# GLA scores as packed 64x64 products with a state per chunk, and low parts and rotary sums on VectorE

## The chip, the cores and the metric

The kernel runs on one core of one Trainium2 chip. The metric is the device time of one execution in microseconds. Before the change three runs took 1275.5, 1276.38 and 1276.91 us (median 1276.38).

## The reference

One layer of a streaming encoder over 1024 frames of width 1024, batch 1. A conditioning vector gives shift, scale and gate for two sublayers. The first sublayer mixes tokens:

```
u    = LN0(x) * (1 + scale1) + shift1
proj = u @ w_in                                 # 3600 columns: rq rk rv rg gq gk gv gg glr
ro   = head_norm(retention(rope(rq), rope(rk), rv)) * silu(rg)   # 4 heads, dk = dv = 128
go   = head_norm(gla(gq, gk, gv, log_a)) * silu(gg)              # 4 heads, dk = 64, dv = 128
x    = LN1(alpha * x + gate1 * ([ro | go] @ w_out))
```

The second is a feed-forward layer with a squared relu. All mixing is causal by chunks of 64 frames. The part that the change rewrites most is gated linear attention (GLA). With b the cumulative log gate inside a chunk, for each chunk and head:

```
A[t, s] = sum_d q[t, d] k[s, d] exp(-|b[t, d] - b[s, d]|)        # inside a chunk, both ways
o       = A @ v + (q * exp(b)) @ state
state   = exp(b_last) * state + (k * exp(b_last - b)).T @ v
```

The decay differs for each channel d, so A is not one matrix product.

## The kernel before

All arithmetic is float32. Large matmuls are computed from a high part (float32r, written by a cast on ScalarE, L205) and a low part (the rest, a subtraction, L206), three matmuls for one product (L211 to L213). The helper `split` does both; its argument `lo_eng` names the engine of the low part, GpSimd where it is missing. Before the change the low parts of w_in (`wl`: 52 tiles of 128x512 and 8 of 128x272, L206 called from `load_w`), those of every second half of the input (`ul`, 8 tiles, from `modulate`) and of every first half of w_out (`ol`, 8 tiles, from `load_out`) are on GpSimd.

The sequence is cut into two halves of 512 frames (h), the four GLA heads into two blocks of two heads (blk), which lie on partitions 0 to 63 and 64 to 127. `gla` is thus called four times, each time for 512 frames and two heads, between the projections. It works with tiles of 128 frames, which hold two chunks each. To build A it splits the pairs (t, s) of a tile by levels: at the level of u frames (32, 16, 8, 4, 2, 1) the pairs that lie in the two halves of a block of 2u frames are one product of `qe` and `ke`, both scaled with the exponential of b's distance from the boundary between the halves (E: GpSimd L562 and L563, exponential on ScalarE L564, products on VectorE L566 and L567). `scores` then does 8 matmuls of 64 channels, 128 keys and 128 queries (L544), into one PSUM bank for each head, and VectorE copies what belongs to this level over `am` by a mask (L552, two copies of 128x512 for each level). Two more calls of `scores` come first: one, with `qB` and `kB`, for pairs in which the query's chunk follows the key's (mask C_M64, L554), and one, with q and k, for the diagonal.

The state is kept for each tile of 128 frames. So `qB` and `kB`, scaled towards their own chunk's bounds, are turned by GpSimd into `qI` and `kI`, scaled towards the tile's bounds (L576, L577), with the tile's decay `gdt` (L580). `kI` is transposed and copied out (L583, L585), its product with v gives the update of each tile (L593), VectorE chains the states (L600), and the output is the sum of the product of `qI` with the state (L611) and that of `am` with v (L617).

In retention each of four heads' q and k is rotated: ScalarE copies the projection (L646), VectorE does three products (L647 to L649), GpSimd adds (L650), 16 times in all, and scales q with the decay (L654).

Instructions stand in the program as the functions call each other, but a planner then orders every engine's queue by priority and modelled times before the kernel runs, and gives tags without a fixed number of buffers what room there is. On the chip each engine works through its queue in that order. Weight tiles of w_in share 16 buffers (tag W) for their high and low parts. All loads and stores go through SP's queue.

Of the kernel before, what the change touches and what calls it, by code (L numbers as in the profile page):

```python
# [16 lines left out]
P = 128  # L17
# [21 lines left out]
C_TRI = 128  # L39
C_DEC = 256  # L40
C_QD = C_DEC + 512
C_M64 = C_QD + 512
C_LV = C_M64 + 128
LEVELS = (32, 16, 8, 4, 2, 1)
C_KD = C_LV + 128 * len(LEVELS)
C_N = C_KD + 4


# [3 lines left out]
def shape_constants():  # L52

    half = 64
    inv = (1.0 / (np.float32(10000.0) ** np.linspace(0.0, 1.0, half, dtype=np.float32))).astype(np.float32)
    ang = np.arange(SEQ, dtype=np.float32)[None, :] * inv[:, None]
    cos = np.cos(ang.astype(np.float64)).astype(np.float32)
    sin = np.sin(ang.astype(np.float64)).astype(np.float32)
    cosT = np.concatenate([cos, cos], 0)
    sinT = np.concatenate([sin, -sin], 0)  # L60
    lg = np.log1p(-(2.0 ** (-5.0 - np.arange(4, dtype=np.float64))))
    i = np.arange(P)
    s, t = i[:, None], i[None, :]
# [8 lines left out]
    c[:, C_M64:C_M64 + P] = (s < 64) & (t >= 64)  # L72
    for n, h in enumerate(LEVELS):
        c[:, C_LV + P * n:C_LV + P * (n + 1)] = (s // (2 * h) == t // (2 * h)) & (s // h != t // h)
# [5 lines left out]
def layer_kernel(ctx: ExitStack, tc, x, c, w_ada, b_ada, w_in, ret_norm_w, gla_gate_w, gla_gate_b,  # L80
# [55 lines left out]
    def table(o, n=P):  # L136
        return keep[:, o:o + n] if o < C_DEC else cst1[:, o - C_DEC:o - C_DEC + n]
# [212 lines left out]
    def load_w(ranges, kk):  # L350

        n = sum(r[1] for r in ranges)
        hi, lo = [], []
        for k in range(0, NK, kk):
            w = stage((P, kk, n))
            o = 0
            for a, m in ranges:
                nc.sync.dma_start(out=w[:, :, o:o + m], in_=wi[:, k:k + kk, a:a + m])
                o += m
            th, tl = S((P, kk, n), F32R, "wh"), S((P, kk, n), F32R, "wl")  # L360
            split(w, th, tl)
# [170 lines left out]
        return q, k, b, eb, qB, kB  # L532

    def gla(blk, h, gv, q, k, b, eb, qB, kB):
        am = [S(n="am"), S(n="am")]

        def scores(ka, qa, put):

            heads = [slice(64 * hd, 64 * hd + 64) for hd in range(2)]
            tiles = [slice(j * P, (j + 1) * P) for j in range(4)]  # L540
            pss = [mxt(), mxt()]
            for o in tiles:
                for hd in range(2):
                    T.matmul(pss[hd][:, o], lhsT=ka[heads[hd], o], rhs=qa[heads[hd], o], start=True, stop=True)  # L544
            for hd in range(2):
                put(am[hd].rearrange("p (j t) -> p j t", t=P), pss[hd].rearrange("p (j t) -> p j t", t=P))

        def cmask(o):
            return table(o).unsqueeze(1).broadcast_to([P, 4, P])

        def overlay(o):
            return lambda a, ps: V.copy_predicated(out=a, mask=cmask(o).bitcast(U32), data=ps)  # L552

        scores(kB, qB, lambda a, ps: V.tensor_tensor(out=a, in0=ps, in1=cmask(C_M64), op=ALU.mult))  # L554
        scores(k, q, overlay(C_ID))
        for n, u in enumerate(LEVELS):
            e = S(n="E")
            bv = b.rearrange("p (n u) -> p n u", u=2 * u)
            ev = e.rearrange("p (n u) -> p n u", u=2 * u)
            nb = HALF // (2 * u)  # L560
            ref = bv[:, :, u - 1:u].broadcast_to([P, nb, u])
            G.tensor_tensor(out=ev[:, :, :u], in0=ref, in1=bv[:, :, :u], op=ALU.subtract)  # L562
            G.tensor_tensor(out=ev[:, :, u:], in0=bv[:, :, u:], in1=ref, op=ALU.subtract)  # L563
            A.activation(e, e, AF.Exp)  # L564
# [3 lines left out]
            scores(ke, qe, overlay(C_LV + P * n))  # L568


        eb4 = eb.rearrange("p (j c u) -> p j c u", c=2, u=CHUNK)
        qI, kI = S(n="qI"), S(n="kI")
        for src, dst, c0 in ((qB, qI, 0), (kB, kI, 1)):
            s4 = src.rearrange("p (j c u) -> p j c u", c=2, u=CHUNK)
            d4 = dst.rearrange("p (j c u) -> p j c u", c=2, u=CHUNK)
            G.tensor_copy(out=d4[:, :, c0, :], in_=s4[:, :, c0, :])  # L576
            G.tensor_tensor(out=d4[:, :, 1 - c0, :], in0=s4[:, :, 1 - c0, :],  # L577
                            in1=eb4[:, :, c0, CHUNK - 1:CHUNK].broadcast_to([P, 4, CHUNK]), op=ALU.mult)
        dt = small(4, "gdt", bufs=4)
        G.tensor_tensor(out=dt, in0=eb4[:, :, 0, CHUNK - 1], in1=eb4[:, :, 1, CHUNK - 1], op=ALU.mult)  # L580
        kp = mxt()
        for j in range(4):
            T.transpose(out=kp[:, j * P:(j + 1) * P], in_=kI[:, j * P:(j + 1) * P], identity=ident)  # L583
        kt = S(n="kt")
        A.copy(out=kt, in_=kp)  # L585

        steps = range(4 if h == 0 else 3)
        before = [gstate[blk]]
        up = mxt((P, 4, P))
        for j in steps:  # L590
            vt = gv[2 * h + j // 2][:, j % 2, :]
            for hd in range(2):
                T.matmul(up[64 * hd:64 * hd + 64, j, :], lhsT=kt[:, j * P + 64 * hd:j * P + 64 * hd + 64],  # L593
                         rhs=vt[:, hd * P:(hd + 1) * P], start=True, stop=True)
        states = S((P, 4, P), n="states")
        for j in steps:
            if before[j] is None:
                V.tensor_copy(out=states[:, j, :], in_=up[:, j, :])
            else:
                V.scalar_tensor_tensor(out=states[:, j, :], in0=before[j], scalar=dt[:, j:j + 1], in1=up[:, j, :],  # L600
                                       op0=ALU.mult, op1=ALU.add)
            before.append(states[:, j, :])
        gstate[blk] = before[-1]
        op = [mxt((P, 4, P)), mxt((P, 4, P))]

        with_state = [j for j in range(4) if before[j] is not None]
        for j in with_state:
            o = slice(j * P, (j + 1) * P)
            for hd in range(2):
                r = slice(64 * hd, 64 * hd + 64)  # L610
                T.matmul(op[hd][:, j, :], lhsT=qI[r, o], rhs=before[j][r, :], start=j == with_state[0], stop=False,  # L611
                         skip_group_check=True)
        for hd in range(2):
            for j in range(4):
                o = slice(j * P, (j + 1) * P)
                vt = gv[2 * h + j // 2][:, j % 2, :]
                T.matmul(op[hd][:, j, :], lhsT=am[hd][:, o], rhs=vt[:, hd * P:(hd + 1) * P], start=False, stop=j == 3,  # L617
                         skip_group_check=True)
# [176 lines left out]
    def load_out():  # L795
        for k in OUT_ORDER:
            for q in range(2):
# [480 lines left out]
```

## Time and profile before

| | |
|---|---|
| median of 3 runs | 1276.38 us |
| the profiled execution | 1275.61 us |
| its span, first to last instruction | 1273.8 us |
| TensorE matmul busy | 1187.6 us (93%) |
| VectorE busy | 965.2 us (76%) |
| ScalarE busy | 496.4 us (39%) |
| GpSimd busy | 301.0 us (24%) |

The profile is one execution; the span leaves out 1.8 us around it. PE is TensorE, PEld its weight loads, DVE VectorE, ACT ScalarE, POOL GpSimd. A matmul of float32 operands leaves two records, one of float32r operands one. In the rows, `x48 | 31.7, 724 | 2.4 <-PE mx L544 2.2` says: 48 instructions, 31.7 us busy in all, 724 ns the mean of one, 2.4 us of idle time before them, most of which ended with a result of TensorE from L544. Where instructions overlap at their ends, the busy time is less than count times mean.

### The profile page before, as it was taken

Reading aid. Unit: us, or ns where it says so; the run is one execution under the profiler, and the core shown is the slowest. Engines: PE = TensorE matmul, PEld = TensorE weight load, DVE = VectorE, ACT = ScalarE, POOL = GpSimd, SP = SyncE. Lnnn points to the kernel's source line nnn. Section 1 sums busy time; section 2 is a strip of 40 time slices with the busy share of each in tenths; the row PEclk is TensorE's granted clock in tenths of the full one; section 3 lists DMA queues with packets and bytes.
Section 4 is the critical chain, followed back from the end, with each engine's and each line's share of the span. In section 5 each row is a group of like instructions: output and inputs, shape, how many; then the busy total and the mean of one; then the engine's idle time right before and its main releaser. Section 6 shows DMA issues by size and latency. Waiting matters only on the chain. (4 is left out here: it accounts for less than half of the span.)

```text
span 1273.8 us, 18210 instructions
## 1 busy us (share of the span) xinstructions
PE 1187.6 (93%) x6491; PEld 993.7 (78%) x6491; DVE 965.2 (76%) x1778; ACT 496.4 (39%) x879; POOL 301.0 (24%) x253
## 2 busy tenths in 40 slices
PE   4899899879899989999998999999999999999995
PEld 1588789667887979988886887888887788888784
DVE  6884876798757585379889978876657786897996
ACT  4424332122121323223475446665655443441222
POOL 1333442463324423000000000000002222242336
PEclk9899989889999999999999999999999999999998
DMA  9685220100011032227124768676464455458632
GB/s 313 207 269 200 83 59 5 38 25 26 9 50 34 21 105 65 77 77 246 53 93 149 245 203 300 232 248 207 149 220 164 142 190 186 134 192 284 233 124 100
DMA packets 124124, 183.31 MB, mean 144 GB/s; under 512 B 12337, under 2 KB 52482, under 8 KB 124034
## 3 DMA queue, kind: packets, MB, share of 16 engines
q1 hardware_dynamic: 124034, 182.16, 43.0%
q8 instruction: 51, 0.84, 0.3%
q14 instruction: 39, 0.32, 0.1%
HBM read 137.02 MB, written 45.09 MB: 143 GB/s over the span
## 5 line engine op out<-in xcount | busy, mean ns | idle before, releaser
L211 PE MATMUL pj<-wh,uh 128*128 128x256 f32 (+1 forms) x512 | 146.5, 287 | 0.3 <-ACT wh L205 0.3
L212 PE MATMUL pj<-wl,uh 128*128 128x256 f32 (+1 forms) x512 | 145.9, 285 | 0.3 <-POOL wl L206 0.3
L213 PE MATMUL pj<-wh,ul 128*128 128x256 f32 (+1 forms) x512 | 146.1, 286 | 0.0
L206 POOL TENSOR_TENSOR al<-rh,ah 128x512 fp32r<-128x512 f32 x17 | 26.7, 1571 | 468.0 <-ACT w1h L205 399.4
L206 POOL TENSOR_TENSOR wl<-st,wh 128x512 fp32r<-128x512 f32 (+1 forms) x60 | 78.2, 1320 | 190.3 <-ACT wh L205 118.9
L211 PE MATMUL pj<-uhp,w1h 128*128 128x512 f32 x256 | 100.2, 393 | 2.0 <-ACT w1h L205 1.1
L211 PE MATMUL pj<-bh,ah 128*128 128x512 f32 x256 | 99.8, 391 | 1.5 <-DVE qv L181 0.8
L212 PE MATMUL pj<-ulp,w1h 128*128 128x512 f32 x256 | 100.0, 391 | 0.0
L213 PE MATMUL pj<-uhp,w1l 128*128 128x512 f32 x256 | 99.9, 391 | 0.0
L212 PE MATMUL pj<-bl,ah 128*128 128x512 f32 x256 | 99.6, 389 | 0.0
L213 PE MATMUL pj<-bh,al 128*128 128x512 f32 x256 | 99.6, 389 | 0.0
L211 PEld LDWEIGHTS pj<-wh,uh 128*128 128x128 f32 x512 | 98.0, 192 | 1.3 <-ACT wh L205 0.7
L212 PEld LDWEIGHTS pj<-wl,uh 128*128 128x128 f32 x512 | 98.2, 192 | 0.9 <-POOL wl L206 0.5
L213 PEld LDWEIGHTS pj<-wh,ul 128*128 128x128 f32 x512 | 98.2, 192 | 0.4 <-issue 0.2
L211 PE MATMUL mx<-uhp,w1h 128*128 128x512 f32 x192 | 75.1, 392 | 2.7 <-ACT w1h L205 2.7
L211 PE MATMUL mx<-bh,ah 128*128 128x512 f32 x192 | 75.4, 394 | 2.1 <-ACT bh L205 1.2
L212 PE MATMUL mx<-bl,ah 128*128 128x512 f32 x192 | 75.6, 394 | 1.1 <-POOL bl L206 0.9
L213 PE MATMUL mx<-bh,al 128*128 128x512 f32 x192 | 75.5, 393 | 0.0
L213 PE MATMUL mx<-uhp,w1l 128*128 128x512 f32 x192 | 75.3, 393 | 0.0
L212 PE MATMUL mx<-ulp,w1h 128*128 128x512 f32 x192 | 75.3, 392 | 0.0
L212 PE MATMUL pj<-ul,wh 128*128 128x512 f32 x176 | 71.1, 406 | 4.3 <-DVE ul L206 2.6
L211 PE MATMUL pj<-uh,wh 128*128 128x512 f32 x176 | 72.0, 411 | 2.7 <-ACT uh L205 2.7
(266 smaller groups left out, 3014.5 us busy)
## 6 DMA issues: line engine op xcount, KB each, us to landing
raw<-in_w_ff SPq DMA_DIRECT2D x140, 256.0 KB, 4.2
ada<-in_w_ada SPq DMA_DIRECT2D x96, 256.0 KB, 5.4
rh<-hid SPq DMA_DIRECT2D x84, 256.0 KB, 3.7
hid<-c SPq DMA_DIRECT2D x54, 256.0 KB, 2.3
st<-in_w_in SPq DMA_DIRECT2D x52, 256.0 KB, 3.0
hid<-m SPq DMA_DIRECT2D x30, 256.0 KB, 2.2
hid<-kl SPq DMA_DIRECT2D x28, 256.0 KB, 3.1
hid<-kh SPq DMA_DIRECT2D x28, 256.0 KB, 2.7
```

The lines of the kernel that those rows point to most:

```text
L206: (lo_eng or G).tensor_tensor(out=lo, in0=src, in1=hi.bitcast(F32), op=ALU.subtract)
L211: T.matmul(ps, lhsT=lh, rhs=rh, start=first, stop=False, skip_group_check=partial)
L212: T.matmul(ps, lhsT=lh, rhs=rl, start=False, stop=False, skip_group_check=partial)
L213: T.matmul(ps, lhsT=ll, rhs=rh, start=False, stop=last, skip_group_check=partial)
```

## The change

- `scores`: 16 matmuls of 64 channels, 64 keys and 64 queries, one for each chunk and head; head picks the rows of the array, the chunk's place in its tile the columns. `am` is one tile of 128 x (2 heads, 4 tiles, 64 queries) with the keys of both chunks on the partitions. Six overlays by masks of 64 columns remain; the diagonal's call comes first and ScalarE copies it; the call for pairs of different chunks is gone, its mask too.
- The state is kept for each chunk: 8 updates and 8 states for 512 frames (7 in the second half) with the decay `eb` at the chunk's last frame; `qI`, `kI` and `gdt` are gone, `qB` and `kB` take their place.
- The product of `am` with v is done for each chunk and for 32 queries at a time.
- The low parts of w_in, w_out and the input, and the rotary sums, are on VectorE.

```diff
     def gla(blk, h, gv, q, k, b, eb, qB, kB):
-        am = [S(n="am"), S(n="am")]
+        am = S((P, 2, 4, CHUNK), n="am")
+        rows = [slice(CHUNK * i, CHUNK * i + CHUNK) for i in range(2)]
...
             pss = [mxt(), mxt()]
-            for o in tiles:
+            for j in range(4):
                 for hd in range(2):
-                    T.matmul(pss[hd][:, o], lhsT=ka[heads[hd], o], rhs=qa[heads[hd], o], start=True, stop=True)
+                    for ch in range(2):
+                        o = cols(2 * j + ch)
+                        T.matmul(pss[hd][rows[ch], cols(j)], lhsT=ka[rows[hd], o], rhs=qa[rows[hd], o], start=True,
+                                 stop=True)
...
-        scores(kB, qB, lambda a, ps: V.tensor_tensor(out=a, in0=ps, in1=cmask(C_M64), op=ALU.mult))
-        scores(k, q, overlay(C_ID))
+        scores(k, q, lambda a, ps: A.copy(out=a, in_=ps))
...
-        up = mxt((P, 4, P))
-        for j in steps:
+        up = [mxt((P, 4, P)), mxt((P, 4, P))]
+        for n in steps:
+            j, ch = n // 2, n % 2
             for hd in range(2):
-                T.matmul(up[64 * hd:64 * hd + 64, j, :], lhsT=kt[:, j * P + 64 * hd:j * P + 64 * hd + 64],
+                T.matmul(up[ch][rows[hd], j, :], lhsT=kt[rows[ch], j * P + CHUNK * hd:j * P + CHUNK * hd + CHUNK],
...
+        for n in with_state:
             for hd in range(2):
+                T.matmul(op[hd][rows[n % 2], n // 2, :], lhsT=qB[rows[hd], cols(n)], rhs=before[n][rows[hd], :],
+                         start=n in with_state[:2], stop=False, skip_group_check=True)
         for hd in range(2):
             for j in range(4):
-                T.matmul(op[hd][:, j, :], lhsT=am[hd][:, o], rhs=vt[:, hd * P:(hd + 1) * P], start=False, stop=j == 3,
+                for t in range(0, CHUNK, 32):
+                    for ch in range(2):
+                        T.matmul(op[hd][CHUNK * ch + t:CHUNK * ch + t + 32, j, :], lhsT=am[rows[ch], hd, j, t:t + 32],
+                                 rhs=ve(j, hd, ch), start=False, stop=j == 3, skip_group_check=True)
...
-        split(u, uh[k][h], ul[k][h], lo_eng=(V, G)[h])
+        split(u, uh[k][h], ul[k][h], lo_eng=V)
...
-            split(w, th, tl)
+            split(w, th, tl, lo_eng=V)
...
-                G.tensor_tensor(out=t1, in0=t1, in1=t2, op=ALU.add)
+                V.tensor_tensor(out=t1, in0=t1, in1=t2, op=ALU.add)
...
-                split(w, oh[k][q], ol[k][q], lo_eng=(G, V)[q])
+                split(w, oh[k][q], ol[k][q], lo_eng=V)
```

## Rows read from the trace of the kernel before

**Rows 1.** Stretches of the span: window, its length, busy us of each engine, granted clock, DMA.
```profile
0.00:128.00 128.00, 103.17 (x514) 74.80 (x515) 88.64 (x147) 53.27 (x97) 40.50 (x39) 0.96 0.74 246
128.00:310.00 182.00, 156.62 (x1298) 136.62 (x1297) 141.38 (x257) 47.68 (x81) 83.05 (x93) 0.93 0.13 39
310.00:512.00 202.00, 187.82 (x1342) 175.20 (x1342) 136.55 (x334) 47.95 (x82) 70.37 (x48) 0.99 0.17 49
512.00:1273.80 761.80, 739.95 (x3343) 607.04 (x3341) 598.62 (x1042) 347.48 (x620) 107.04 (x73) 0.99 0.52 177
```

**Rows 2.** Waits of TensorE, 128 to 310 us: total us, times, longest.
```profile
PE mx L544 <- DVE ke L567: 24.8, 17, 8.2
```

**Rows 3.** Waits of TensorE, 0 to 128 us.
```profile
PE mx L263 <- DVE bs L200: 5.4, 1, 5.4
...
PE mx L263 <- DVE acc L238: 1.9, 1, 1.9
```

**Rows 4.** Waits of TensorE, 310 to 512 us.
```profile
PE mx L663 <- POOL t L650: 3.1, 1, 3.1
```

**Rows 5.** Timeline of the first GLA call: start, length, engine, line, records.
```profile
151.14 1.16 PE L544 MATMUL mx<-qe,ke 64*128 64x128 f32 x16 [0.34 <-DVE ke L567]
...
155.58 1.09 PE L593 MATMUL mx<-v,kt 128*64 128x128 f32 x16
...
157.27 1.05 PE L611 MATMUL mx<-states,qI 64*128 64x128 f32 x12
...
158.26 2.05 PE L617 MATMUL mx<-v,am 128*128 128x128 f32 x16
```

**Rows 6.** Groups of VectorE, 128 to 310 us: busy us, mean ns, idle before.
```profile
L552 DVE COPY_PREDICATED am<-cst,mx 128x512 f32<-128x512 uint32 x48 | 31.7, 724 | 2.4 <-PE mx L544 2.2
L566 DVE TENSOR_TENSOR qe<-gqk,E 128x512 f32<-128x512 f32 x24 | 19.9, 831 | 4.2 <-ACT E L564 4.2
L567 DVE TENSOR_TENSOR ke<-gqk,E 128x512 f32<-128x512 f32 x24 | 19.1, 797 | 0.0
L238 DVE SCALAR_TENSOR_TENSOR acc<-ada,keep,acc 128x512 f32<-128x512 f32 x14 | 13.5, 967 | 0.1
L648 DVE TENSOR_TENSOR t<-p,rope 64x512 f32<-64x512 f32 x4 | 5.7, 1416 | 0.1
...
L554 DVE TENSOR_TENSOR am<-mx,cst 128x512 f32<-128x512 f32 x8 | 5.1, 680 | 0.9 <-PE mx L544 0.9
...
L600 DVE SCALAR_TENSOR_TENSOR states<-states,gdt,mx 128x128 f32<-128x128 f32 x12 | 4.2, 348 | 1.7 <-PE mx L593 1.4
```

**Rows 7.** Single lines, whole span: shortest, median and longest of one, in ns.
```profile
L206 DVE TENSOR_TENSOR ol<-st,oh x8: 677/688/922, 452.6 to 511.3; 128x512 fp32r<-128x512 f32 x8
...
L736 DVE TENSOR_TENSOR mix<-sg,ro x16: 418/420/427, 496.1 to 536.3; 128x256 f32<-128x256 f32 x16
...
L238 DVE SCALAR_TENSOR_TENSOR acc<-ada,keep,acc x71: 735/752/1656, 19.2 to 779.8; 128x512 f32<-128x512 f32 x71
...
L648 DVE TENSOR_TENSOR t<-p,rope x16: 686/1661/1691, 264.9 to 427.9; 64x512 f32<-64x512 f32 x16
```

**Rows 8.** Groups of GpSimd, 0 to 512 us.
```profile
L206 POOL TENSOR_TENSOR wl<-st,wh 128x512 fp32r<-128x512 f32 x52 | 70.8, 1379 | 165.7 <-ACT wh L205 111.3 <-PE pj L212 54.0
L650 POOL TENSOR_TENSOR t<-t,t 128x512 f32<-128x512 f32 x16 | 25.0, 1565 | 21.3 <-DVE t L649 21.3
...
L577 POOL TENSOR_TENSOR kI<-kB,eb 128x256 f32<-128x256 f32 x4 | 3.4, 839 | 0.0
L576 POOL COPY kI<-kB 128x256 f32<-128x256 f32 x4 | 3.2, 795 | 7.3 <-DVE qe L566 7.3
```

**Rows 9.** Timeline of VectorE around its rotary products.
```profile
276.38 1.65 DVE L648 TENSOR_TENSOR t<-p,rope 64x512 f32<-64x512 f32 x1
...
282.88 1.10 DVE L567 TENSOR_TENSOR ke<-gqk,E 128x512 f32<-128x512 f32 x1
```

**Rows 10.** Waits of GpSimd, 128 to 310 us.
```profile
POOL wl L206 <- ACT wh L205: 43.7, 7, 12.0
...
POOL wl L206 <- PE pj L212: 10.5, 1, 10.5
```

More of the change, by code (lines that the diff above doesn't have):

```diff
@@ L41 @@
 C_QD = C_DEC + 512
-C_M64 = C_QD + 512
-C_LV = C_M64 + 128
+C_LV = C_QD + 512
 LEVELS = (32, 16, 8, 4, 2, 1)
-C_KD = C_LV + 128 * len(LEVELS)
+C_KD = C_LV + CHUNK * len(LEVELS)
 C_N = C_KD + 4
@@ L71, in shape_constants @@
         c[:, C_KD + h] = np.exp(lg[h] * (P - 1.0 - i))
[L72 removed]
+    s, t = s % CHUNK, t[:, :CHUNK]
     for n, h in enumerate(LEVELS):
[L74 removed]
+        c[:, C_LV + CHUNK * n:C_LV + CHUNK * (n + 1)] = (s // (2 * h) == t // (2 * h)) & (s // h != t // h)
     gam = [float(np.exp(lg[h] * P)) for h in range(4)]
@@ L534, in gla, with cols @@
     def gla(blk, h, gv, q, k, b, eb, qB, kB):
-        am = [S(n="am"), S(n="am")]
+        am = S((P, 2, 4, CHUNK), n="am")
+        rows = [slice(CHUNK * i, CHUNK * i + CHUNK) for i in range(2)]
+        def cols(n):
+            return slice(CHUNK * n, CHUNK * n + CHUNK)
         def scores(ka, qa, put):
-            heads = [slice(64 * hd, 64 * hd + 64) for hd in range(2)]
-            tiles = [slice(j * P, (j + 1) * P) for j in range(4)]
             pss = [mxt(), mxt()]
-            for o in tiles:
+            for j in range(4):
                 for hd in range(2):
-                    T.matmul(pss[hd][:, o], lhsT=ka[heads[hd], o], rhs=qa[heads[hd], o], start=True, stop=True)
+                    for ch in range(2):
+                        o = cols(2 * j + ch)
+                        T.matmul(pss[hd][rows[ch], cols(j)], lhsT=ka[rows[hd], o], rhs=qa[rows[hd], o], start=True,
+                                 stop=True)
             for hd in range(2):
-                put(am[hd].rearrange("p (j t) -> p j t", t=P), pss[hd].rearrange("p (j t) -> p j t", t=P))
-        def cmask(o):
-            return table(o).unsqueeze(1).broadcast_to([P, 4, P])
+                put(am[:, hd], pss[hd][:, :4 * CHUNK].rearrange("p (j t) -> p j t", t=CHUNK))
         def overlay(o):
-            return lambda a, ps: V.copy_predicated(out=a, mask=cmask(o).bitcast(U32), data=ps)
-        scores(kB, qB, lambda a, ps: V.tensor_tensor(out=a, in0=ps, in1=cmask(C_M64), op=ALU.mult))
-        scores(k, q, overlay(C_ID))
+            m = table(o, CHUNK).unsqueeze(1).broadcast_to([P, 4, CHUNK]).bitcast(U32)
+            return lambda a, ps: V.copy_predicated(out=a, mask=m, data=ps)
+        scores(k, q, lambda a, ps: A.copy(out=a, in_=ps))
         for n, u in enumerate(LEVELS):
@@ L567, in gla @@
             V.tensor_tensor(out=ke, in0=k, in1=e, op=ALU.mult)
[L568 to L578, printed above, removed]
@@ L579, in gla, with ve @@
-        dt = small(4, "gdt", bufs=4)
-        G.tensor_tensor(out=dt, in0=eb4[:, :, 0, CHUNK - 1], in1=eb4[:, :, 1, CHUNK - 1], op=ALU.mult)
+            scores(ke, qe, overlay(C_LV + CHUNK * n))
         kp = mxt()
         for j in range(4):
-            T.transpose(out=kp[:, j * P:(j + 1) * P], in_=kI[:, j * P:(j + 1) * P], identity=ident)
+            T.transpose(out=kp[:, j * P:(j + 1) * P], in_=kB[:, j * P:(j + 1) * P], identity=ident)
         kt = S(n="kt")
         A.copy(out=kt, in_=kp)
-        steps = range(4 if h == 0 else 3)
+        def ve(j, hd, ch):
+            return gv[2 * h + j // 2][rows[ch], j % 2, hd * P:(hd + 1) * P]
@@ L588, in gla @@
+        steps = range(8 if h == 0 else 7)
         before = [gstate[blk]]
-        up = mxt((P, 4, P))
-        for j in steps:
-            vt = gv[2 * h + j // 2][:, j % 2, :]
+        up = [mxt((P, 4, P)), mxt((P, 4, P))]
+        for n in steps:
+            j, ch = n // 2, n % 2
             for hd in range(2):
-                T.matmul(up[64 * hd:64 * hd + 64, j, :], lhsT=kt[:, j * P + 64 * hd:j * P + 64 * hd + 64],
-                         rhs=vt[:, hd * P:(hd + 1) * P], start=True, stop=True)
@@ L595, in gla @@
[L595 to L598, printed above, removed]
-            else:
-                V.scalar_tensor_tensor(out=states[:, j, :], in0=before[j], scalar=dt[:, j:j + 1], in1=up[:, j, :],
-                                       op0=ALU.mult, op1=ALU.add)
-            before.append(states[:, j, :])
+                T.matmul(up[ch][rows[hd], j, :], lhsT=kt[rows[ch], j * P + CHUNK * hd:j * P + CHUNK * hd + CHUNK],
+                         rhs=ve(j, hd, ch), start=True, stop=True)
@@ L603, in gla @@
+        states = [S((P, 4, P), n="states"), S((P, 4, P), n="states")]
+        for n in steps:
+            new, u = states[n // 4][:, n % 4, :], up[n % 2][:, n // 2, :]
+            if before[n] is None:
+                V.tensor_copy(out=new, in_=u)
+            else:
+                V.scalar_tensor_tensor(out=new, in0=before[n], scalar=eb[:, CHUNK * n + CHUNK - 1:CHUNK * n + CHUNK],
+                                       in1=u, op0=ALU.mult, op1=ALU.add)
+            before.append(new)
         gstate[blk] = before[-1]
@@ L604, in gla @@
         op = [mxt((P, 4, P)), mxt((P, 4, P))]
-        with_state = [j for j in range(4) if before[j] is not None]
-        for j in with_state:
-            o = slice(j * P, (j + 1) * P)
+        with_state = [n for n in range(8) if before[n] is not None]
+        for n in with_state:
             for hd in range(2):
-                r = slice(64 * hd, 64 * hd + 64)
-                T.matmul(op[hd][:, j, :], lhsT=qI[r, o], rhs=before[j][r, :], start=j == with_state[0], stop=False,
-                         skip_group_check=True)
+                T.matmul(op[hd][rows[n % 2], n // 2, :], lhsT=qB[rows[hd], cols(n)], rhs=before[n][rows[hd], :],
+                         start=n in with_state[:2], stop=False, skip_group_check=True)
```

3 lines of the change are left out of this document (removed).

## The prediction

> **What bounds the kernel now.** I read the stretches first: busy time of each engine in four parts of the span [rows 1]. From 512 us on TensorE works 740.0 of 761.8 us and nothing that the change touches runs there; what can move lies before. From 0 to 128 us the DMA engines are 74% busy with weights and TensorE works 103.2 of 128. From 128 to 310 us, where the four GLA calls run, TensorE works 156.6 of 182, VectorE 141.4, and the granted clock is 0.93, a mean over the two levels of 2.4 and 1.2 GHz. From 310 to 512 us (retention, gates) TensorE works 187.8 of 202. So TensorE sets the pace, and its holes are what can be had beside its own work. The waits of TensorE say who makes them: in the GLA stretch one cause, 24.8 us behind `ke` of L567, which VectorE writes [rows 2]; at the start the statistics and sums of VectorE, 5.4 and 1.9 us [rows 3]; later little, of which 3.1 us are behind the rotary sum that GpSimd writes [rows 4]. The GLA stretch is therefore bound by two engines in turn: TensorE when the projections between the score matmuls last, VectorE when they run out.
>
> **TensorE's part of the change.** The timeline shows the present cost of each matmul group [rows 5]; an f32 matmul leaves two records. One scores call: 16 records, 1.16 us. The 16 full 128x128 records of `am` take 2.05 us, 0.11 us each; records in two row tiles (L544, L611) or two column tiles (L593) come at half of that, 0.055 us, so tiles of one kind do overlap. No row shows row and column tiles together. If all four overlap, a scores call has 32 records, 8 on each tile, each on 64 moving columns instead of 128, so 0.055 us a tile: 0.44 us, with 0.35 us for the first record's start and the last one's run about 0.8 us. State matmuls (32 records on 4 tiles, 8 x 0.11 + 0.35) take 1.2 us, updates the same, the `am` product (64 records on 4 tiles of 128 columns, 16 x 0.11 + 0.35) 2.1 us. A GLA call has now 8 x 1.16 + 2.05 + 1.09 + 1.05 = 13.5 us and would have 7 x 0.8 + 2.1 + 1.2 + 1.2 = 10.1 us: 3.4 us less, 13.6 us less in four calls. Bounds: with pairs only, as the rows show them, a record costs half a step, 0.027 us in a scores call and 0.054 elsewhere, with 0.27 us for the last one's run: 1.13 us a scores call, the others 3.7, 2.0 and 2.0, so 15.6 us a call, 8.4 us more in all; if each new record cost the 0.054 us that L593 takes, 14.0 + 7.7 = 21.7 us a call, 33 us more. I take four tiles, since each kind of pair overlaps by the full factor; -13.6, ends -16 (a start that costs nothing beside that run) and +33.
>
> One rule bears on the `am` product alone. The rows with two row tiles write a bank for each head, while the new product writes both row tiles into one bank `op[hd]`. The Trainium skill, TensorEngine Tiling (Array Packing), section Restrictions and Gotchas, says that different row tiles cannot access one PSUM bank at the same time. No trace here shows it either way. By that rule the product would have column pairs alone, 3.7 us for 2.1, and the sum would be 6.4 us higher.
>
> **VectorE's part in the GLA stretch** [rows 6, 7].
> - Overlays: 56 of L552 now, 48 on the level masks with 31.7 us busy and 8 alike on the identity, so 37 us. 48 remain at half the columns: a 128x512 operation takes 0.687 us and a 128x256 one 0.420, so 0.27 less than 0.66 busy, 0.39 x 48 = 18.7. With the cross-chunk scores (8 of L554, 5.1 us) gone: -23.5. The first write of `am` goes to ScalarE, 8 copies, under 0.6 us each, on an engine that works 47.7 of 182 us [rows 1]: nothing on the path.
> - States: 30 steps instead of 14, at 0.348: +5.6.
> - The low parts of 15 weight tiles, 0.687 each: +10.3; four rotary sums: +2.7.
> - Relief: operations of VectorE on two SBUF tiles grow while GpSimd works. `ol` takes 0.677 to 0.922 us, L238 0.752 in the median, but here `qe` means 0.831, `ke` 0.797, L238 0.967 and the rotary L648 1.416. The excess over 0.69 (0.75 for L238) is 3.4 + 2.6 + 3.0 + 2.9 = 11.9 us in these four rows, an estimated 16 with the others. GpSimd loses 15 x 1.38 = 21 us of low parts, 6 of sums and, at some 0.8 each, 13 for 16 operations on `qI` and `kI`, of its 83 [rows 1, 8], about half, so I take -8 (from 0, if what is left collides as often, to -16).
> Together -13 us of 141, with ends -21 and -5. The cycle of one level shortens from about 3.0 us (qe, ke, two overlays) to 2.2, and `kt` no longer waits for `kI`.
>
> Both engines that bound this stretch thus get about 13 us lighter, and so does the stretch: -13.6, and some 2 us for `ke` stalls that shrink faster than the cover, the 8.2 us one above all: a rotary product of 1.65 us and, 6 us later, the `ke` that ended it at 1.10 us stand in VectorE's order just before [rows 9]. I put -16 there.
>
> **The start (0 to 128 us).** VectorE gets 23 weight tiles (15 of 0.687, 8 smaller of about 0.42) and 8 low parts of the input: +19 us on 88.6; relief on L238 and its own `ul`, about -8. It has 39 us idle, and the DMAs of the weights lie beside it; the hiding work is TensorE's 103 us. Cover is thin only where TensorE waits for VectorE already [rows 3], where some six low parts, 4 us, can stand in front; the relief can give back as much as 2: +1, ends -2 and +4.
>
> **After the GLA calls (310 to 512 us).** 22 weight tiles, 12 rotary sums and 8 tiles of w_out: 42 x 0.687 = +29 us on 136.6, less the relief (12 of the 16 groups of rotary products lie here; the excess of L648 alone, 0.73 a group, makes 9 of it, its neighbours and the gates an estimated 9), which I put at -18: +11 on an engine with 65 us idle. TensorE's wait for the sum, 3.1 us, goes, since it takes 0.69 instead of 1.56 us [rows 8]; the low parts may now stand behind norms. 0, ends -6 and +6.
>
> The load of the mask tables shrinks by 0.26 MB; no other DMA is added, removed or moved past another on purpose. A planner orders the whole program anew, so small shifts anywhere, after 512 us too, are in the range.
>
> **Sum.** The profiled execution took 1275.6 us, its span 1273.8. 1275.6 + 1 - 16 + 0 = 1260.6; the median of the three runs is 0.8 us above that execution, so 1261 us, on its own from 1252 to 1269.
>
> **Rivals.**
> 1. Head of the line (slower). VectorE takes its instructions in order. A low part waits for the cast on ScalarE, which waits until a matmul frees the buffer. GpSimd stood 43.7 us behind that cast and 10.5 us behind the matmul in the GLA stretch, 3.6 us for each of 15 tiles [rows 10]; there it held up little, here it would hold `ke`. For: the planner goes by modelled times. Against: it can place the low part later, and only VectorE's 41 idle us show how far the plan is off. It decides from 16 / 15 = 1.1 us a tile; at 1.6 us, +24 - 16 gives 1284 us. Chance 0.15.
> 2. Only pairs overlap: TensorE +8.4, the `ke` stalls down from 25 to about 15 by the shorter cycle, so -2 there and with the start -1 in all: 1275 us. For: no row shows more than two tiles at once. Against: nothing in the rows ties row and column tiles together. Chance 0.13.
> 3. The packed records do not overlap at all: +33, less some 12 of stalls, +1: 1298 us. Against it: all tiled rows overlap. Chance 0.04.
> 4. The `am` product alone overlaps in pairs: 3.7 for 2.1 us in each of four calls, +6.4, so 1267 us. For: it alone writes both row tiles into one bank. Against: they write other partitions of it. Chance 0.12. The rule of the Trainium skill named above speaks for this case.
> 5. The stalls go almost wholly: -13.6 and 12 of the 24.8 us, with the clock back at 1.00 in part: 1248 us. For: half of the cause, contention at the rotary products, is taken away. Against: the projections that cover stalls get no longer. Chance 0.10.
>
> **How the numbers follow.** The forecast has 0.46. Smaller differences than 0.2% (2.6 us) can't be told from no change by a measurement of this kernel. Faster: the forecast, 4, 5 and a third of 2, together 0.72. Within 0.2%: half of 2 and some of 1, 0.09. Slower: 3, most of 1, the rest of 2, 0.19. The range 1244 to 1282 leaves out part of 1, all of 3 and the lower tail of 5, about 0.17.
>
> **What would show it.** Packing: L544 with 32 records in about 0.8 us; near 1.1 it is rival 2, near 2 rival 3. The `am` product: 64 records in about 2.1 us, 3.7 for rival 4. VectorE: overlays near 0.45 us, low parts near 0.69, `qe`, `ke` and L648 nearer to 0.69, and in the GLA stretch its busy time 13 us lower. Rival 1: waits of VectorE for the cast `wh`, none of which stand in the profile before. The stretch from the first GLA scores to the last `am` product should be 16 us shorter, and what follows it the same length; if it is shorter than that by the packing alone, or the gain lies after 512 us, the reasoning is wrong, even with the time right.

## The result and the profile after

The changed kernel takes 1233.16 us in the median of four runs (1230.3 to 1237.34), the kernel before 1275.94 us beside it (1275.08 to 1276.91): ratio 0.9656, 95% interval 0.9638 to 0.9674. The direction was right. The gain is 42.8 us where 15 were forecast, and the time lies below the range that was given. The profiled execution after took 1232.21 us, its span 1230.4.

To see where the time went, the span is cut at the same matmuls in both kernels: the first decay sum of the GLA calls, the last `am` product, the first product with w_out. Retention and gates reach beyond 512 us, so these are not quite the stretches of [rows 1]. First the kernel before, with the columns of [rows 1]:

```profile
0.00:125.90 125.90, 101.42 (x502) 73.14 (x502) 86.64 (x144) 51.87 (x95) 40.50 (x39) 0.96 0.76 250
125.90:306.10 180.20, 154.48 (x1291) 135.06 (x1292) 139.97 (x249) 47.48 (x80) 81.76 (x92) 0.93 0.14 39
306.10:535.10 229.00, 214.82 (x1552) 201.36 (x1551) 146.81 (x360) 54.56 (x94) 71.66 (x49) 0.99 0.18 52
535.10:1273.80 738.70, 716.85 (x3150) 584.09 (x3148) 591.79 (x1027) 342.46 (x611) 107.04 (x73) 0.99 0.53 180
```

And the kernel after:

```profile
0.00:122.10 122.10, 101.75 (x509) 75.20 (x509) 89.04 (x175) 51.65 (x95) 0.76 (x8) 0.97 0.77 256
122.10:278.10 156.00, 142.64 (x2013) 117.85 (x2013) 130.10 (x268) 48.20 (x89) 46.03 (x54) 0.97 0.16 47
278.10:488.10 210.00, 207.03 (x1531) 195.33 (x1528) 148.15 (x402) 53.39 (x93) 9.06 (x6) 1.00 0.18 55
488.10:1230.40 742.30, 718.71 (x3150) 585.44 (x3148) 592.17 (x1027) 342.18 (x611) 106.21 (x73) 0.99 0.53 179
```

The second number is the length, the third TensorE's busy time; their difference is TensorE's idle time. By stretch the change is worth -3.8, -24.2, -19.0 and +3.6 us. TensorE's busy time falls by 17.4 us over the span, 11.8 of them in the GLA stretch and 7.8 in the third, and its idle time by 26.0 (from 24.5, 25.7, 14.2 and 21.9 to 20.4, 13.4, 3.0 and 23.6). VectorE took over 19, 13 and 29 us of work by the prediction's count and is busy for only 2.4 and 1.3 us more in the first and third stretch. The matmuls of `gla` named below fall by more than 11.8 us, from 59.5 busy to 41.8; the stretch falls by less because 18 more records of projections lie in it (605 for 587), which the third stretch no longer has. They start 0.23 us apart, so an estimated 4 us of the third stretch's gain is work that only moved. The granted clock rises a little where the idle time falls: 0.93 to 0.97 with the GLA calls, 0.99 to 1.00 behind them.

The packing is seen in the timeline of TensorE in the first GLA call (start, length, line, records; it answers to [rows 5]). In the new kernel L549 is `scores` (L544 before), L589 the updates, L607 the products with the states, L613 the one of `am`:

```profile
140.31 0.69 PE L549 MATMUL mx<-qe,ke 64*64 64x64 f32 x32
...
148.64 1.10 PE L589 MATMUL mx<-v,kt 64*64 64x128 f32 x32
...
151.05 0.45 PE L607 MATMUL mx<-states,qB 64*64 64x128 f32 x8
151.98 0.45 PE L607 MATMUL mx<-states,qB 64*64 64x128 f32 x8
...
153.28 1.95 PE L613 MATMUL mx<-v,am 64*32 64x128 f32 x64
```

A scores call takes 0.69 us (0.8 forecast, 1.16 before), the `am` product 1.95 (2.1 forecast): four tiles overlap, and rivals 2, 3 and 4 fall. For rival 4 spoke a rule of the Trainium skill, TensorEngine Tiling (Array Packing), section Restrictions and Gotchas: different row tiles cannot access one PSUM bank at the same time. L613 writes both row tiles into one bank, and its 64 records come 0.03 us apart, where one kind of pair alone gave 0.055 [rows 5]; the measurement decides. The products with the states come in groups of 8, one every 0.93 us, with projections between them; TensorE does not idle there.

The waits of TensorE at the start, in the GLA stretch and in the third one (total us, times, longest) answer to [rows 2 to 4]:

```profile
PE mx L262 <- DVE bs L199: 5.6, 1, 5.6
...
PE mx L549 <- DVE ke L570: 11.8, 8, 5.7
PE mx L549 <- ACT E L567: 1.2, 1, 1.2
...
PE mx L715 <- DVE mix L732: 1.5, 1, 1.5
PE mx L691 <- DVE rs L662: 0.7, 1, 0.7
PE mx L659 <- DVE t L646: 0.3, 1, 0.3
```

At the start the wait for the statistics stayed. The `ke` stalls went from 24.8 to 11.8 us. Behind the GLA calls the kernel before had more waits than the 3.1 us of [rows 4]; up to its 535 us they were:

```profile
PE mx L695 <- DVE rs L666: 4.4, 1, 4.4
PE mx L663 <- POOL t L650: 3.1, 1, 3.1
PE mx L719 <- DVE mix L736: 2.9, 2, 2.0
PE mx L679 <- DVE ro L704: 1.6, 1, 1.6
```

All of these shrink, three of them on instructions that the change does not touch. The groups of VectorE say why. Before, from 306 to 535 us (busy us, mean ns, idle before):

```profile
L648 DVE TENSOR_TENSOR t<-p,rope 64x512 f32<-64x512 f32 x12 | 17.1, 1427 | 0.2
L800 DVE SCALAR_TENSOR_TENSOR st<-st,keep,g 128x512 f32<-128x512 f32 x16 | 14.3, 910 | 3.8 <-DMA st<-in_w_out 3.7 <-issue 0.2
...
L704 DVE TENSOR_SCALAR ro<-mx,rmv,rrs 128x128 f32<-128x128 f32 x32 | 10.9, 404 | 0.5
L736 DVE TENSOR_TENSOR mix<-sg,go 128x256 f32<-128x256 f32 x16 | 10.8, 718 | 12.3 <-ACT sg L733 12.3
L206 DVE TENSOR_TENSOR ml<-mx,mh 128x512 fp32r<-128x512 f32 x14 | 9.2, 686 | 17.0 <-PE pj L212 10.6 <-PE mx L719 6.3
```

After, from 278 to 488 us, and under it the single line L732 (shortest, median and longest in ns):

```profile
L205 DVE TENSOR_TENSOR wl<-st,wh 128x512 fp32r<-128x512 f32 x22 | 15.2, 690 | 4.0 <-ACT wh L204 3.4
L796 DVE SCALAR_TENSOR_TENSOR st<-st,keep,g 128x512 f32<-128x512 f32 x16 | 11.6, 748 | 3.0 <-DMA st<-in_w_out 2.8
L644 DVE TENSOR_TENSOR t<-p,rope 64x512 f32<-64x512 f32 x12 | 11.2, 937 | 0.2
L700 DVE TENSOR_SCALAR ro<-mx,rmv,rrs 128x128 f32<-128x128 f32 x32 | 10.9, 404 | 0.4
...
L205 DVE TENSOR_TENSOR ml<-mx,mh 128x512 fp32r<-128x512 f32 x14 | 9.1, 684 | 0.1
...
L732 DVE TENSOR_TENSOR mix<-sg,go x16: 415/418/426, 388.6 to 439.7; 128x256 f32<-128x256 f32 x16
```

Instructions with two inputs in SBUF were long before, as [rows 7] have it, and are shorter now (L648 to L644, which still meets `qd`, L800 to L796, L736 to L732). Those with an input in PSUM (`ro`, `ml`) did not change. At the start one with a single input tile in SBUF, `uf`, was over 1 us at times, each time beside low parts on GpSimd, and is no longer; before and after:

```profile
L342 DVE TENSOR_SCALAR uf<-xT,keep x16: 533/546/1629, 27.6 to 69.8; 128x512 f32<-128x512 f32 x16
```

```profile
L341 DVE TENSOR_SCALAR uf<-xT,keep x16: 538/542/547, 27.3 to 63.5; 128x512 f32<-128x512 f32 x16
```

A low part on VectorE takes 0.69 us and waits little for its cast.

In the GLA stretch after (it answers to [rows 6]):

```profile
L556 DVE COPY_PREDICATED am<-cst,mx 128x256 f32<-128x256 uint32 x48 | 18.5, 438 | 0.9 <-PE mx L549 0.8
L569 DVE TENSOR_TENSOR qe<-gqk,E 128x512 f32<-128x512 f32 x24 | 18.3, 762 | 0.7 <-ACT E L567 0.7
L570 DVE TENSOR_TENSOR ke<-gqk,E 128x512 f32<-128x512 f32 x24 | 18.3, 762 | 0.0
...
L205 DVE TENSOR_TENSOR wl<-st,wh 128x512 fp32r<-128x512 f32 x15 | 10.3, 713 | 2.7 <-ACT wh L204 2.5 <-ACT v L450 0.2
L597 DVE SCALAR_TENSOR_TENSOR states<-states,eb,mx 128x128 f32<-128x128 f32 x28 | 9.7, 348 | 2.8 <-PE mx L589 1.8
```

### The profile page after: what moved, and what is told of

It reads as the page before. It is cut to its first block, busy times and chain, and to the rows that moved or that the text cites. A ratio compares the mean times of both kernels' runs of the same rounds, so it can differ in the third digit from the quotient of the medians.

```text
span 1230.4 us, 19534 instructions
## 1 busy us (share of the span) xinstructions
PE 1170.1 (95%) x7195; PEld 973.8 (79%) x7195; DVE 959.5 (78%) x1870; ACT 495.4 (40%) x887; POOL 162.1 (13%) x141
## 5 line engine op out<-in xcount | busy, mean ns | idle before, releaser
L205 DVE TENSOR_TENSOR w1l<-raw,w1h 128x512 fp32r<-128x512 f32 x80 | 54.7, 686 | 25.6 <-ACT w1h L204 16.1
L204 ACT CAST ah<-rh 128x512 fp32r<-128x512 f32 x84 | 51.9, 618 | 51.3 <-PE pj L211 21.4
```

## The experiments

Two theories of what the moves off GpSimd bring:

- K, contention: while a GpSimd instruction with two inputs runs, an instruction of VectorE that reads SBUF (with two inputs, mostly) stands. Measure for it: the excess, the time by which VectorE's instructions over 0.5 us lasted longer than the fastest tenth of the same form (operation and operands), summed where it is over 0.1 us.
- Q, the queue: E of the GLA levels stands on GpSimd behind low parts, and so behind their casts.

All times are in us; the stretches are cut at the same matmuls as above (here exactly at the first decay sum, 0.3 us later than above), idle is that of TensorE, excess that of VectorE. Medians come from four to ten runs, stretches from the one execution that was profiled; four runs of the changed kernel span 7 us, so a difference of 1 or 2 us in a stretch is not taken as shown.

| kernel | median | GLA: length, idle, excess | third: length, idle, excess |
|---|---|---|---|
| before | 1275.9 | 179.9, 25.4, 20.2 | 229.0, 14.2, 29.1 |
| e1_pack | 1270.6 | 171.4, 26.6, 22.5 | 224.8, 13.8, 27.5 |
| e2_engines | 1248.4 | 169.0, 16.5, 12.8 | 211.8, 1.9, 5.1 |
| after | 1233.2 | 155.8, 13.1, 16.8 | 210.0, 3.0, 4.7 |
| e3_rot | 1240.5 | 157.0, 15.5, 18.2 | 216.9, 8.3, 11.5 |
| e4_wl | 1259.1 | 174.1, 24.3, 21.9 | 218.3, 8.8, 18.2 |
| e5_blk | 1237.7 | 161.4, 14.5, 17.1 | 210.7, 3.7, 4.6 |
| e6_dummy | 1281.6 | 179.3, 28.2, 29.2 | 220.0, 9.9, 22.8 |
| e7_eight_v | 1251.6 | 164.2, 19.4, 22.6 | 218.3, 8.6, 18.2 |
| e8_eight_g | 1241.9 | 165.3, 18.1, 17.5 | 210.0, 3.1, 4.7 |
| e9_qd | 1230.4 | 156.5, 11.7, 14.9 | 207.2, 1.3, 0.0 |
| e10_state | 1226.8 | 151.2, 16.5, 16.1 | 210.5, 2.3, 4.5 |
| e11_E | 1244.1 | 165.7, 12.9, 2.6 | 211.1, 9.2, 5.0 |
| e12_both | 1225.8 | 150.7, 16.1, 16.4 | 208.0, 0.7, 0.0 |

**The two halves of the change.** The GLA part alone, with the engines as before:

```diff
-        split(u, uh[k][h], ul[k][h], lo_eng=V)
+        split(u, uh[k][h], ul[k][h], lo_eng=(V, G)[h])
...
-            split(w, th, tl, lo_eng=V)
+            split(w, th, tl)
...
-                V.tensor_tensor(out=t1, in0=t1, in1=t2, op=ALU.add)
+                G.tensor_tensor(out=t1, in0=t1, in1=t2, op=ALU.add)
...
-                split(w, oh[k][q], ol[k][q], lo_eng=V)
+                split(w, oh[k][q], ol[k][q], lo_eng=(G, V)[q])
```

> Only the GLA part of the change; the low parts and the rotary sums stay on GpSimd. Theory A (two parts that add: packing acts in the GLA stretch, the engine moves act at the start and in the retention stretch): about 1276 - 22 = 1254 us, with the first GLA scores near 131 us and the stretch from the last am product to the out-projection near 229 us, as before. Rival B (the packing brings all, since a shorter GLA stretch lets the planner order what follows better): about 1236 us, with that later stretch near 210 us. Rival C (the engine moves bring nearly all by less contention): above 1262 us.

Measured: 1270.58 against 1277.42 us, ratio 0.9951 (0.9933 to 0.9969). And the moves alone, the kernel before with the same four lines as they are after:

> Only the engine moves (low parts of w_in, w_out and the input and the rotary sums on VectorE); GLA as before the change. Theory A: about 1276 - 23 = 1253 us, the later stretch near 211 us, the GLA stretch about 4 us shorter than its 180. Rival B (all by the packing): 1274 to 1282 us. Rival C (less contention brings nearly all): about 1240 us, with qe and ke at 0.72 us or less and the GLA stretch near 165 us.

Measured: 1248.43 us, 0.9773 (0.9752 to 0.9794). The packing alone takes 9.7 us of TensorE's work out of the GLA stretch and no idle time; though VectorE has 15.7 us less to do there, the stalls stay. The moves alone take 8.9 us of idle time there and 12.3 in the third stretch, with VectorE busy for 5.0 us more in the first of the two. So the stalls were not made by the sum of VectorE's work, but by something that the moves changed. By their ratios the halves are worth 6 and 29 us alone and 44 together: the packing pays 15 once the engines are changed (1248.4 to 1233.2). Of the three theories e1_pack leaves rival C alone; e2_engines lies between C's number (1240) and A's (1253).

**Which of the moves.** After, with the rotary sums back on GpSimd, and after with the 60 low parts of w_in back there:

```diff
-                V.tensor_tensor(out=t1, in0=t1, in1=t2, op=ALU.add)
+                G.tensor_tensor(out=t1, in0=t1, in1=t2, op=ALU.add)
```

> The changed kernel with the 16 rotary sums alone back on GpSimd. Theory A1 (the retention stretch was held by the sums' way through GpSimd, 1.56 us each behind other work there): most of its 19 us come back, about 1245 to 1250 us. Rival A2 (it was held by contention and queueing of the weights' low parts): within 4 us of the changed kernel, 1230 to 1237 us.

```diff
-            split(w, th, tl, lo_eng=V)
+            split(w, th, tl)
```

> The changed kernel with the low parts of the 60 w_in tiles alone back on GpSimd. Theory A1: about 1237 to 1240 us (start and contention in the GLA stretch come back, the retention stretch stays near 210 us). Rival A2: 1250 us or more, the retention stretch near 225 us, L644 and L645 back above 1.2 and 0.9 us.

Measured: 1240.5 us (0.9716, 0.9689 to 0.9743) and 1259.12 us (0.9857, 0.9842 to 0.9873). The sums are worth 7 us, nearly all in the third stretch, where their return brings 6.8 us of excess and 5.3 of idle time. The low parts of w_in are worth 26 us, 18.3 in the GLA stretch and 8.3 in the third. So both matter in the third stretch; A1 had the sums too dear and the low parts too cheap, A2 the sums too cheap.

**Waiting, or working, on GpSimd.** After, with GpSimd made to wait for every cast of w_in and then to copy 8 columns; and after, with GpSimd computing each low part once more into a tile that nobody reads:

```diff
...
             th, tl = S((P, kk, n), F32R, "wh"), S((P, kk, n), F32R, "wl")
             split(w, th, tl, lo_eng=V)
+            G.tensor_copy(out=junk, in_=th[:, 0, 0:8].bitcast(F32))
```

> The changed kernel, and GpSimd copies 8 columns of the high part of each of the 60 w_in tiles into a spare tile, an addition that no output needs: it stands in GpSimd's queue where the low parts stood and waits for the same casts, but is short and has one input. Theory Q (the low parts held GpSimd's queue: while one waited for its cast, the subtractions E behind it waited too): the GLA stretch goes from 156 to about 170 us, E of the second and third call starts 12 us or more after b, the whole about 1250 us. Theory K (the low parts on GpSimd slowed VectorE by running beside it): within 4 us of the changed kernel, 1230 to 1237 us.

```diff
...
             split(w, th, tl, lo_eng=V)
+            G.tensor_tensor(out=junk[:, :kk * n].rearrange("p (k c) -> p k c", k=kk), in0=w, in1=th.bitcast(F32), op=ALU.subtract)
```

> The changed kernel, and GpSimd computes the 60 low parts of w_in once more into a spare tile, an addition that no output needs: the same waits and the full length beside VectorE. Theory Q: about as the run with short copies, 1250 us, with up to 6 us more for the longer instructions in front of E. Theory K: 1255 us or more, qe and ke at 0.86 us as with the low parts back on GpSimd, while the run with short copies stays near 1233.

Measured: 1237.66 us (0.9676, 0.9639 to 0.9713) and 1281.6 us (1.0025, 1.0004 to 1.0046). The same place in the queue, behind the same casts, and 4.5 us (by the intervals not told apart from after) or 48 us. VectorE's low parts in the third stretch, with the short copies and then with the full ones:

```profile
L205 DVE TENSOR_TENSOR wl<-st,wh 128x512 fp32r<-128x512 f32 x22 | 15.2, 691 | 4.0 <-ACT wh L204 3.4
```

```profile
L205 DVE TENSOR_TENSOR wl<-st,wh 128x512 fp32r<-128x512 f32 x22 | 22.2, 1022 | 4.1 <-ACT wh L204 3.5 <-PE pj L212 0.4
```

How the collision goes is seen in four low parts of the second kernel, on VectorE and on GpSimd:

```profile
180.21 5.78 DVE L205 TENSOR_TENSOR wl<-st,wh 128x512 fp32r<-128x512 f32 x4 [1.53 <-ACT wh L204]
...
180.26 6.86 POOL L362 TENSOR_TENSOR junk<-st,wh 128x512 f32<-128x512 f32 x4 [7.74 <-ACT wh L204]
```

The first, begun before GpSimd's, takes 0.69 us, each further one 1.7, as long as GpSimd's: it stands until the other has ended. Of the 60 low parts there 33 took up to 0.69 us, 19 took 1.67 to 1.78, 8 lay between. The Trainium skill, SBUF — State Buffer, section Who interferes with whom, says this: a VectorE instruction with two SBUF inputs shares a read interface with GpSimd, and the one that comes second blocks for the whole instruction. Trace and page agree. In the third stretch GpSimd has little else to do, and the second kernel has 18.2 us more excess, 6.2 more idle time, and is 9.3 us longer. Its GpSimd also holds the loaded weights for longer, so that the loads of w_in wait for it there for 8.9 us in SP's queue; but none of TensorE's three waits in that stretch (3.9, 3.9 and 2.1 us) ends with a weight: they end with chains of VectorE (`rs`, `t`) and with `rkt` of ScalarE. Theory K holds there.

**The GLA stretch.** In the second and third call of the kernel before four low parts (keys rq and rk of heads 0 and 1) stand on GpSimd between `b` and E. All low parts of w_in but these eight back on GpSimd, and these eight alone:

```diff
...
-                loaded[u] = load_w(*W[u])
+                loaded[u] = load_w(*W[u], V if u[0] in ("rq", "rk") and u[1] < 2 else G)
```

> The low parts of w_in on GpSimd but for eight tiles (the rotary heads 0 and 1), those that stood in front of E of the second and third GLA call; the rest of the change is in. Theory Q: of the 26 us that all 60 tiles cost, these eight give back 12 to 15: 1245 us, the GLA stretch about 160 us. Theory K: 8 of 60 tiles, 3 us: 1256 us.

```diff
...
-                loaded[u] = load_w(*W[u])
+                loaded[u] = load_w(*W[u], G if u[0] in ("rq", "rk") and u[1] < 2 else V)
```

> The changed kernel with these eight tiles alone back on GpSimd. Theory Q: 12 to 15 us slower than the changed kernel, 1246 us, E of the second and third call 14 us or more after b, the GLA stretch about 170 us, the stretch after it as in the changed kernel. Theory K: 3 us slower, 1236 us.

Measured: 1251.57 us (0.9786, 0.9749 to 0.9823) and 1241.88 us (0.972, 0.9674 to 0.9766). The eight tiles alone make the GLA stretch 9.5 us longer (165.3 for 155.8), with all others on GpSimd 9.9 us (e4_wl 174.1, e7_eight_v 164.2); the other stretches of e8_eight_g lie within 1.4 us of after. The excess moves by 0.7, so it is not the collision. Of the 9.5 us 5.0 are idle time; the other 4.5 are TensorE's busy time, at a granted clock of 0.94 instead of 0.97. Both medians lie between the numbers of the two theories (Q 1245 and 1246, K 1256 and 1236): Q named the place, and put it at more than it costs. GpSimd's timeline in the second call, first with the eight tiles there, then with short copies in their place (e5_blk), then after:

```profile
165.85 5.20 POOL L205 TENSOR_TENSOR wl<-st,wh 128x512 fp32r<-128x512 f32 x4 [7.74 <-PE pj L211]
171.01 1.06 POOL L565 TENSOR_TENSOR E<-b 128x256 f32<-128x256 f32 x1
```

```profile
165.90 2.52 POOL L362 COPY junk<-wh 128x8 f32<-128x8 f32 x4 [7.43 <-ACT wh L204]
168.37 0.61 POOL L567 TENSOR_TENSOR E<-b 128x256 f32<-128x256 f32 x1
```

```profile
157.02 1.04 POOL L525 TENSOR_TENSOR ek<-b 128x512 f32<-128x512 f32 x1 [16.63 <-DVE rt L172]
158.02 0.61 POOL L565 TENSOR_TENSOR E<-b 128x256 f32<-128x256 f32 x1
```

`b` is ready at 157 us in all three. The first `qe` starts at 173.8, 170.5 and 170.8, and from `b` to the end of the `am` product the call takes 40.9, 36.7 and 36.7 us. VectorE has other work until 170 us, so an E at 168 costs nothing and an E at 171, with the exponential behind it, 4 us. The kernel before had it at 178.8, 17 us behind `b`, and its call took 44.3:

```profile
173.70 5.18 POOL L206 TENSOR_TENSOR wl<-st,wh 128x512 fp32r<-128x512 f32 x4 [10.52 <-PE pj L212]
178.83 1.06 POOL L562 TENSOR_TENSOR E<-b 128x256 f32<-128x256 f32 x1
```

In the third call a late E costs more: from `b` to the end 39.8 us with the eight tiles, 37.9 with the short copies, 35.0 after. With the eight tiles VectorE stands for E there:

```profile
216.31 1.03 DVE L569 TENSOR_TENSOR qe<-gqk,E 128x512 f32<-128x512 f32 x1 [4.33 <-ACT E L567]
```

So in the second and third call Q is right, but it is not the wait alone: wait and length of the four low parts together pass the slack, which is some 10 us in the second. In the fourth call E starts 14.6 us behind `b` even after, behind two `qd`; e9_qd, below, has it 1.5 us behind `b`, and the call takes 44.2 us instead of 44.3. A late E costs nothing where VectorE has other work.

**What is left.** The scaling `qd` on VectorE too:

```diff
-                    G.tensor_tensor(out=qd.rearrange("p (j t) -> p j t", t=P), in0=t1.rearrange("p (j t) -> p j t", t=P),
+                    V.tensor_tensor(out=qd.rearrange("p (j t) -> p j t", t=P), in0=t1.rearrange("p (j t) -> p j t", t=P),
```

> The changed kernel, with the scaling of the retention queries (qd, 8 operations on 128x512) on VectorE too, so that GpSimd has no two-input work left beside the retention. Now each takes GpSimd about 1.55 us, and the product of VectorE beside it 937 ns where the same one elsewhere takes 686. Theory K (what a two-input operation of GpSimd costs is the time by which it lengthens VectorE's beside it): VectorE gets 8 x 0.69 = 5.5 us and loses about as much of excess, so VectorE's busy time in the retention stays within 3 us of 148, and TensorE, which idles there only 3 us, can gain no more than that: about 1231 us (-2, from 1229 to 1234). Rival M (the moved work is a load on VectorE like any other, and the retention stretch was near its limit): busy 153 us, idle of TensorE up by 3 to 5, about 1237 us.

Measured: 1230.42 us (0.9635, 0.9611 to 0.9659), not told apart from after. In its profile K's numbers stand: VectorE took 6 of the 8 operations in the third stretch and is busy for 1.1 us less there; idle time 1.3 for 3.0.

The transpose, the updates and the chain of states ahead of the scores:

```diff
-        scores(k, q, lambda a, ps: A.copy(out=a, in_=ps))
-        for n, u in enumerate(LEVELS):
...
         kp = mxt()
...
         gstate[blk] = before[-1]
         op = [mxt((P, 4, P)), mxt((P, 4, P))]
 
+        scores(k, q, lambda a, ps: A.copy(out=a, in_=ps))
+        for n, u in enumerate(LEVELS):
...
```

> The changed kernel, with the transpose of kB, the updates and the chain of states ahead of the scores instead of behind them in each GLA call; the instructions are the same. Now a call ends about 9 us after its last ke: the states follow on VectorE, then the state products, then the am product. If what is left of TensorE's idle time in the GLA stretch (13 us) comes from the chain of VectorE at a call's end, it shrinks by 1 to 2 us a call: 1226 to 1230 us. If it comes from the levels (E, exponential, qe, ke, product in turn), the states ahead only put VectorE's 30 steps (0.35 us each, 2.6 us a call) before the first level: no change or up to 10 us more, 1233 to 1243 us.

Measured: 1226.81 us (0.9607, 0.9593 to 0.9622), faster than after, within the first of the two ranges, but not for its reason: the time was in TensorE's busy time, 142.7 us before this edit and 134.6 with it, and not in its idle time, which rose there from 13.1 to 16.5. About half of it is in the products with the states, after and then here, in the GLA stretch:

```profile
L607 PE MATMUL mx<-states,qB 64*64 64x128 f32 x120 | 8.3, 294 | 0.0
```

```profile
L607 PE MATMUL mx<-states,qB 64*64 64x128 f32 x120 | 4.4, 271 | 0.0
```

The records are the same. In the first call of after they come in four groups (0.44 and three times 0.45 us) between projections; here they come in one:

```profile
149.72 1.05 PE L607 MATMUL mx<-states,qB 64*64 64x128 f32 x28
```

The first projection behind such a group takes 0.38 or 0.39 us, those that follow it 0.28. What the rest of the 8.1 us is was not split up.

Both subtractions of E on VectorE:

```diff
-            G.tensor_tensor(out=ev[:, :, :u], in0=ref, in1=bv[:, :, :u], op=ALU.subtract)
-            G.tensor_tensor(out=ev[:, :, u:], in0=bv[:, :, u:], in1=ref, op=ALU.subtract)
+            V.tensor_tensor(out=ev[:, :, :u], in0=ref, in1=bv[:, :, :u], op=ALU.subtract)
+            V.tensor_tensor(out=ev[:, :, u:], in0=bv[:, :, u:], in1=ref, op=ALU.subtract)
```

> The changed kernel, with both subtractions of the level exponents E (6 levels, 2 operations each on 128x256, in four calls: 48 operations) on VectorE; GpSimd keeps ek, qI, kI and qd. VectorE gets 48 x 0.42 = 20 us in the GLA stretch. Theory K (relief about pays for moved work, as it did for the low parts and the rotary sums): qe, ke and the sums there lie at 0.76 us now against 0.69, an excess of about 0.07 on some 150 two-input operations, so at most 11 us come back: VectorE busy from 130 to 139 or more, and TensorE's idle time there goes from 13 to between 13 and 22: 1233 to 1242 us. Theory Q (the wait in GpSimd's queue is what counted): E follows at once on VectorE, every level loses a hand-over, and the stretch gets shorter by 5 us or more: 1228 us.

Measured: 1244.07 us (0.9744, 0.9712 to 0.9775), above both numbers. The 20 us of work brought back 14.2 of excess (VectorE busy +3.2), yet the span is 10.7 us longer: over the span TensorE is busy for 5.2 us more and idle for 5.5 more. The idle time lies in the third stretch (9.2 for 3.0), one wait above all:

```profile
PE mx L691 <- DVE rs L662: 6.9, 1, 6.9
```

Why the order led there was not tried. Not every move off GpSimd pays, even where the collision goes.

Last, both edits that came out ahead of after:

> The changed kernel with both edits that came out ahead of it: the states ahead of the scores, and qd on VectorE. Each alone: 1226.81 and 1230.42 us against 1233.16. They lie in different stretches (the states in the GLA calls, where TensorE had 142.7 us of work and then 134.6; qd in the retention, where it idled 3.0 us and then 1.3), so they should add: -6.4 and -2.7 give 1224 us (1221 to 1227). If the gain of qd alone was only the order that the planner found, 1227 us or more.

Measured: 1225.83 us (0.9604, 0.9579 to 0.9629), inside the range and ahead of after; from e10_state alone it cannot be told. So whether the two gains add is not shown by the times. In the profile both are there (150.7 us in the GLA stretch, 0.7 of idle time in the third).

## Why the prediction was wrong

- **TensorE's part of the change**: -13.6 forecast; the groups it priced fell by 17.7 (59.5 to 41.8), the stretch's busy time by 11.8, and by 9.7 with the packing alone. The mechanism was right. Its size was off mainly in the base: the prediction's sum gives the four calls 54 us before, where 59.5 were busy, in a stretch with a granted clock of 0.93; for after it gives 40.4, and 41.8 were measured.
- **The start**: +1 forecast, -3.8 measured. The relief of L238 and `ul` was put at 8 us; the excess fell from 15.4 to 0.8. VectorE grew by 2.4 us instead of 11.
- **VectorE's part in the GLA stretch**: -13 forecast, -9.9 measured. The relief there was less than the 8 taken, 3.4 us: E stayed on GpSimd, and with E moved as well (e11_E) the excess there falls from 16.8 to 2.6.
- **The stalls of the GLA stretch**: -2 forecast, -12.3 of idle time measured. Here the prediction failed first. It gave [rows 2] to VectorE, which writes `ke`, and of GpSimd's waits in [rows 10] it said that they held up little. In fact E stood behind them, 17 us after `b` in the second and third call, and `ke` needs E. The release named last in a row of waits was only the last link. e8_eight_g shows what that place is worth: eight tiles back in it, 9.5 us, 5.0 of them idle time. How the rest of the 12.3 divides is not shown; in the kernel before, VectorE itself stood for E for 4.2 us only [rows 6]. Rival 5 had the direction and about the size of the stalls, 12 us, for another cause.
- **After the GLA calls**: 0 forecast, -19.0 measured, the largest miss. The prediction set 29 us of moved work against 18 of relief and judged VectorE by that sum. The excess fell by 24.4, and the sum was not the measure: 12.0 of TensorE's 14.2 us of idle time lay behind short chains of VectorE and GpSimd, in which an instruction of VectorE took up to 1.7 us where it collided. With the collisions mostly gone 3.0 us are left, at a busy time of VectorE that is 1.3 us higher. The other 7.8 of the 19.0 us are TensorE's busy time, of which an estimated 4 only moved into the stretch before. And only one wait was priced, the sum's 3.1 us, where four made 12.
- **Rival 1**, a wait for the cast at the head of VectorE's queue: it exists, 2.5 us in the GLA stretch and 3.4 behind it, but no stall of TensorE in these two stretches ends with a low part.
- **The clock** was given a part in rival 5 alone. One minus the granted clock, times the length and summed over the stretches, falls from 24.8 to 16.8 us: by this estimate 8 us of TensorE's 17.4. It went with the idle time: e6_dummy has 28.2 us idle in its GLA stretch at 0.90, after 13.1 at 0.97.
- **After 512 us**: nothing forecast, +3.6 measured; from 1.8 to 7.6 us in every kernel here but e12_both (739.0 us, 0.3 more than before). No run was made to find the cause; it stays open.

The direction was right, with the packing that the forecast was built on; that the gain came out nearly three times as large was not foreseen. The chance was spent on whether the packing would work, and the larger half lay in what GpSimd's instructions cost others: by the time during which VectorE stands (start, third stretch), and by their length in front of E (GLA calls).

## What to carry to other kernels

A two-input operation on GpSimd is not free because GpSimd is idle: look for VectorE's groups whose mean lies above their shortest (those with two inputs in SBUF first), sum that excess, and set it against the work to be moved; here the moves alone (e2_engines) put 61 us of work on VectorE, and its busy time rose from 965.2 to 974.7. A wait row names the last link only: follow it one engine further, to what stood in front of that engine's input. And judge an engine that is not full by the length of its chains in front of the bound engine, not by its busy sum.

## What the hardware showed

- Four 64x64 tiles of f32 overlap: 32 records in 0.69 us. Two row tiles into one bank of PSUM, on different partitions, do too: 64 records in 1.95 us.
- A collision on SBUF stops one engine until the other's instruction has ended: low parts of 0.69 us took 1.67 to 1.78.
- Small groups of matmuls on 64x64 tiles between projections on the whole array cost TensorE busy time: the 120 records of L607 took 8.3 us in groups of 4 and 8 and 4.4 in one group a call, and a projection behind such a group took 0.38 us instead of 0.28.
